# A hybrid token-mixer trunk on one core: four ScalarE operations by head in place of one VectorE operation in layer 0's x scans

## The chip, the core and the metric

One core of one Trainium2 chip. The metric is the device time of one execution in microseconds, the median of several runs. The engines: TensorE (PE; its weight loads are PEld), VectorE (DVE), ScalarE (ACT), GpSimd (POOL) and SyncE (SP), each with a queue of its own that it works off in order.

## What is computed

A trunk of two layers over 512 latent tokens (x) and 256 context tokens (c) of width 1024. A layer normalises, runs four token mixers side by side (pooling, Mamba-2 SSD in both directions, gated DeltaNet in both directions, Fourier), gates and merges them, and then retrieves experts (PEER): 8 heads choose 16 of 16384 single-neuron experts per token. The context goes first; its final states start the scans of x. The two scans, cut to what matters:

```
ssd:   acs    = cumsum(dt * a)                                  # per head, in a chunk
       decay  = exp(where(lower, acs_i - acs_j, -inf))
       y      = (C B^T * decay) (x dt) + C S exp(acs)
delta: gc     = cumsum(g);  decay = exp(where(lower, gc_i - gc_j, -inf))
       a_mat  = where(strict, (k k^T) * decay * beta, 0);  ia = a_mat + I
       u      = solve(ia, v * beta);  w = solve(ia, k * (beta * exp(gc)))
       attn   = (q k^T) * decay;      kdec = k * exp(glast - gc)
       v_new  = u - w S;  o = (q exp(gc)) S + attn v_new;  S = S exp(glast) + kdec^T v_new
```

## The kernel before

All data is fp32 (128 tokens or features on the partitions); the large projections split both operands into a high and a low part and take three matmuls. Instructions are written through the class K; every engine call goes through one helper (line 150), so that line stands for nearly all of the program in a profile and tiles tell the operations apart. A scheduler lays the written operations into the five queues: by priorities, by when it takes inputs and buffers to be ready, and by "sections" that must follow one another. Nobody writes the final order by hand, so an operation that moves to another engine moves others with it.

A layer runs so: the context's projections and scans, then the x tokens' scans, mixing and output projection (mix_out), then the top-k (peer_front), then the experts. The experts of the two context tiles and of one x tile are gathered row by row: GpSimd fetches 128 rows of a table by an indirect DMA into one of four buffers gat (fetch), VectorE multiplies and sums it (the u table, into gdot: gather_u) or scales it and adds it to a sum gacc (the v table: gather_v). The other three x tiles go through all experts as dense matmuls. In layer 0 the context's 512 gathers are a generator (rows) that tick() advances between the steps of the x scans with low priority. What is left of it runs on to the start of the dense part.

The x scans of layer 0 are recurrent(l=0, NT=4). It writes, in this order: the qkv projections, gdn_norm and the token-major keys and values (kt, vt, stored to DRAM as tok), then eight gdn_A, one for each of 4 chunks and 2 directions, whose matrices are inverted block by block in gdn_inv; the xbc projections, ssd_local per chunk and the SSD state steps; and at last eight delta steps, each of gdn_whole (completes the inverse X), gdn_uw and gdn_step.

The diff touches two places. decay makes exp of differences of log decays: a mask is multiplied by the log decays of four heads into R (128 x 4 x 128), a matmul with the other mask sums them, ScalarE takes the exp:

```
R = self.s2((128, 4, 128))
nc.vector.tensor_tensor(R, la[:, :, None].to_broadcast([128, 4, 128]),
                        in_mask[:, None, :].to_broadcast([128, 4, 128]), op=OP.mult)
```

It is called once in gdn_A, four times in ssd_local (2 directions, 2 groups of heads) and once in gdn_uw (each time with the full x scans). gdn_uw multiplies the keys kt by two factors per token and head into ke and kd: by eb = beta exp(gc) and EX for the forward direction, by EX and eb for the other.

In the trace R is s<-la,masks, the key products are s<-s,eb and s<-s,EX (128x512; EX also scales states). In the dense part, it holds the chosen experts' indices, gp their gates, and gates_all compares indices with iota into one-hot B and A, multiplies A by gp (twice) and hands both to TensorE.

Of the kernel before, what the change touches and what calls it, by code (L numbers as in the profile page):

```python
# [17 lines left out]
AF = mybir.ActivationFunctionType  # L18
OP = mybir.AluOpType
# [165 lines left out]
class K:  # L185
# [363 lines left out]
    def norm_steps(self, x, fm, g, s, hT, keep=None):  # L549
        nc = self.nc  # L550
        NT = len(x)
        T = NT * 128
        hh, hl = hT[:, 0], hT[:, 1]
# [84 lines left out]

    def proj_fm(self, src, unit, h, T, fn):

        ps = [self.p()[:, :T] for _ in range(2)]
        for k2 in range(0, 8, 2):
            wh, wl = self.load_w(src[unit, k2 // 4, :, k2 % 4:k2 % 4 + 2])
            for j in range(2):
                for k in range(2):
                    f = slice(j * 128, (j + 1) * 128)
                    self.mm3(ps[j], (wh[:, k, f], wl[:, k, f]), (h[0][k2 + k], h[1][k2 + k]),
                             k2 + k == 0, k2 + k == 7)
        for j in range(2):
            fn(j, ps[j])  # L650
# [13 lines left out]

    def conv_silu(self, l, tile_i, ps, T, bias):

        nc = self.nc
        w = self.vec[l][:, V_CONV + 5 * tile_i:V_CONV + 5 * tile_i + 5]
        u = self.s2((128, T))
        if bias is None:  # L670
            nc.scalar.activation(u, ps, AF.Copy, scale=w[:, 2:3])
        else:
            nc.scalar.activation(u, ps, AF.Identity, scale=w[:, 2:3], bias=bias)
        for k in (0, 1, 3, 4):
            s = k - 2
            a, b = max(0, -s), T - max(0, s)
            nc.vector.scalar_tensor_tensor(u[:, a:b], ps[:, a + s:b + s], w[:, k:k + 1], u[:, a:b],
                                           op0=OP.mult, op1=OP.add)
        th = self.s2((128, T))
        nc.scalar.activation(th, u, AF.Tanh, scale=0.5)  # L680
        nc.vector.scalar_tensor_tensor(u, th, 1.0, u, op0=OP.add, op1=OP.mult)
        return u
# [60 lines left out]
    def decay(self, la, out_mask, in_mask):  # L743

        nc = self.nc
        R = self.s2((128, 4, 128))
        nc.vector.tensor_tensor(R, la[:, :, None].to_broadcast([128, 4, 128]),
                                in_mask[:, None, :].to_broadcast([128, 4, 128]), op=OP.mult)
        ps = self.p((128, 4, 128))
        nc.tensor.matmul(ps, out_mask, R, start=True, stop=True)  # L750
        E = self.s2((128, 4, 128))
        nc.scalar.activation(E, ps, AF.Exp)
        return E

    def dirs(self, d):
        return ((self.LE, self.GT), (self.GE, self.LT))[d]
# [216 lines left out]
    def gdn_uw(self, c, d, X, kt, vt, kf, qf, la, beta, EX, full):  # L973

        nc = self.nc
        tl = slice(c * 128, (c + 1) * 128)
        ei = EX[:, 0, c, 12 * d + 8:12 * d + 12]
        ew = EX[:, 1, c, 12 * d + 8:12 * d + 12]
        b = beta[:, c, 4 * d:4 * d + 4]

        def bc(a):
            return a[:, :, None].to_broadcast([128, 4, 128])
        ke = self.s2((128, 4, 128))
        kd = self.s2((128, 4, 128))
        eb = self.t([128, 4], "eb", 4)
        if d == 0:
            nc.vector.tensor_mul(eb, ei, b)
            vb = self.s2((128, 4, 128))
            nc.vector.tensor_tensor(vb, vt, bc(b), op=OP.mult)
            nc.vector.tensor_tensor(ke, kt, bc(eb), op=OP.mult)  # L990
            nc.vector.tensor_tensor(kd, kt, bc(ew), op=OP.mult)
        else:
            nc.vector.tensor_mul(eb, ew, b)
            vb = vt
            nc.vector.tensor_tensor(ke, kt, bc(ei), op=OP.mult)
            nc.vector.tensor_tensor(kd, kt, bc(eb), op=OP.mult)
        pu = self.p((128, 4, 128))
        pw = self.p((128, 4, 128))
        for h in range(4):
            nc.tensor.matmul(pu[:, h, :], X[:, h, :], vb[:, h, :], start=True, stop=True)  # L1000
            nc.tensor.matmul(pw[:, h, :], ke[:, h, :], X[:, h, :], start=True, stop=True)
        u = self.s2((128, 4, 128))
        w = self.s2((128, 4, 128))
        nc.scalar.copy(u, pu)
        nc.scalar.copy(w, pw)
        if not full:
            return u, w, kd, None
        inc, exc = self.dirs(d)
        pq = self.p((128, 4, 128))
        for h in range(4):  # L1010
            nc.tensor.matmul(pq[:, h, :], kf[h][:, tl], qf[h][:, tl], start=True, stop=True)
        qm = self.s2((128, 4, 128))
        nc.vector.tensor_tensor(qm, pq, inc[:, None, :].to_broadcast([128, 4, 128]), op=OP.mult)
        at = self.decay(la[:, c, 12 * d + 8:12 * d + 12], exc, inc)
        nc.vector.tensor_tensor(at, at, qm, op=OP.mult)
        if d == 1:
            nc.vector.tensor_tensor(at, at, bc(b), op=OP.mult)
        return u, w, kd, at
# [52 lines left out]
    def recurrent(self, l, h, NT, init, full, F, branch):  # L1071

        T = NT * 128
        win = self.io["w_in"][l]
        dt, la, beta, EX = self.scan_scalars(l, h, NT)
        xbc, qkv = {}, {}
# [78 lines left out]
        for n in range(2 * NT):  # L1155
# [3 lines left out]
            with self.section(sec, steps[-SD]) as step:  # L1159
                X = self.gdn_whole(d * NT + c, d, blocks)  # L1160
                kt, vt = (self.get_state(t, 4) for t in tok[c])
# [912 lines left out]
```

## Time and profile before

| | |
|---|---|
| median of 3 runs | 5746.06 us |
| the runs | 5738.55, 5749.92, 5746.06 us |
| profiled execution, its own time | 5736.66 us |
| its span, first to last instruction | 5734.9 us |
| mean granted clock of TensorE | 0.928 |
| busy over the span: PE, DVE, ACT, POOL | 87%, 74%, 34%, 31% |

Windows are in us from the span's start; a busy time is the time in which at least one instruction of the engine ran. A row of a group has the engine, the operation, out<-in with buffer numbers left out, the shapes and the count, then busy us and the mean ns of one, then the idle time in front of it and what ended it. The chain of waits is followed back from the last instruction to what released each step; "issue" in it is time in which the profile shows nothing that was waited for. In a timeline a row has start, duration, engine and operation, and in brackets the idle time ahead of it.

### The profile page before, as it was taken

To read this page: it belongs to the slowest core of one execution; us is meant where nothing else is said; L and a number is where in the kernel's file an instruction comes from. 1 tells how busy PE (TensorE), PEld (TensorE's weight loads), DVE (VectorE), ACT (ScalarE), POOL (GpSimd) and SP (SyncE) were. 2 spreads that over 40 slices of the span, in tenths; PEclk is the share of its full clock that TensorE was granted. 3 is DMA by queue.
4 is the path that set the end of the run, shared out by engine and by line. 5 is a ranking of instruction groups with operands and counts; after the bars stand their busy time and mean duration, and the time that the engine had idled before them with its cause. 6 is when DMAs were issued, how large, how long until landed. Compare 5 with 4: busy or idle time off the path is not lost.

```text
span 5734.9 us, 76857 instructions
## 1 busy us (share of the span) xinstructions
PE 5001.5 (87%) x26902; PEld 4212.1 (73%) x26902; DVE 4267.5 (74%) x7999; ACT 1951.3 (34%) x3711; POOL 1771.4 (31%) x1290
## 2 busy tenths in 40 slices
PE   8998877988467787699999979999888978999997
PEld 3787755763456676699987867787677978999786
DVE  4665777877788889898777786468566488977777
ACT  2444421321003322254333344233134334533333
POOL 0000344333554575644432210000002445443221
PEclk9999989989678898899999989999999989999999
DMA  6555589888878775699889864434334339988897
GB/s 218 176 166 178 166 299 333 268 274 289 286 261 295 243 238 177 223 366 340 298 314 340 317 202 130 127 104 130 125 120 138 126 117 311 364 304 314 316 333 245
DMA packets 618069, 1372.35 MB, mean 239 GB/s; under 512 B 95568, under 2 KB 229328, under 8 KB 614864
## 3 DMA queue, kind: packets, MB, share of 16 engines
q1 hardware_dynamic: 470224, 830.50, 43.5%
q0 software_dynamic: 147456, 536.94, 27.1%
q8 instruction: 211, 3.46, 0.2%
q14 instruction: 178, 1.46, 0.1%
HBM read 1225.64 MB, written 141.56 MB: 238 GB/s over the span
## 4 chain that ended last, share of the span: by engine, by line
PE 55%; DVE 12%; DMA 10%; issue 9%; POOL 5%; ACT 2%; SPq 0%; POOLq 0%; DVEq 0%; ACTq 0%
PE ps L150 39%; PE pa L150 16%; POOL gat L150 4%; DVE s L150 3%; DMA gat<-in_v,gidx 3%; DMA gat<-in_u,gidx 2%; DVE oh L150 1%; DVE gacc L150 1%; DVE gat L150 1%; DMA dv<-in_v 1%; DMA wraw<-in_w_out 1%; POOL dl L150 1%; DMA a<-acts 1%; DMA wraw<-in_w_in 1%; DVE tki L150 1%
## 5 line engine op out<-in xcount | busy, mean ns | idle before, releaser
L150 POOL DMA_INDIRECT gat<-in_v,gidx x512 | 626.8, 1224 | 1063.9 <-DVE gacc L150 924.0
L150 POOL DMA_INDIRECT gat<-in_u,gidx x512 | 684.2, 1336 | 854.1 <-DVE gat L150 783.4
L150 DVE SCALAR_TENSOR_TENSOR gacc<-gat,gact,gacc 128x1024 f32<-128x1024 f32 x508 | 692.7, 1364 | 93.4 <-DMA gat<-in_v,gidx 88.8
L150 PE MATMUL ps<-hx,dh 128*128 128x384 f32 x2944 | 758.8, 338 | 0.0
L150 DVE SCALAR_TENSOR_TENSOR gat<-gat,hb 128x1024 f32<-128x1024 f32 x512 | 629.7, 1241 | 155.8 <-DMA gat<-in_u,gidx 155.2
L150 PE MATMUL ps<-s,s 128*128 128x128 f32 (+3 forms) x2752 | 422.6, 312 | 159.7 <-issue 81.9
L150 PEld LDWEIGHTS ps<-s,s 128*128 128x128 f32 (+1 forms) x2752 | 378.2, 215 | 231.1 <-issue 122.3
L150 PEld LDWEIGHTS ps<-hx,dh 128*128 128x128 f32 x2944 | 534.9, 190 | 5.8
L150 ACT CAST dh<-du 128x1024 fp32r<-128x1024 f32 x256 | 269.2, 1052 | 723.3 <-PE ps L150 405.0
L150 PE MATMUL ps<-hx,dl 128*128 128x384 f32 x1472 | 495.7, 337 | 2.7 <-POOL dl L150 2.6
L150 DVE TENSOR_TENSOR vl<-dv,vh 128x1024 fp32r<-128x1024 f32 x256 | 313.5, 1225 | 206.9 <-ACT vh L150 206.6
L150 ACT CAST xwhi<-xwraw 128x512 fp32r<-128x512 f32 x352 | 217.7, 620 | 519.6 <-PE pa L150 390.8
L150 ACT CAST vh<-dv 128x1024 fp32r<-128x1024 f32 x256 | 269.3, 1052 | 340.1 <-PE ps L150 232.0
L150 PE MATMUL ps<-hx,whi 128*128 128x512 f32 x1152 | 384.1, 401 | 0.0
L150 PE MATMUL pa<-hx,xwhi 128*128 128x512 f32 x1152 | 376.9, 404 | 6.0 <-DVE ld L150 2.9
L150 ACT CAST whi<-wraw 128x512 fp32r<-128x512 f32 x320 | 197.8, 621 | 478.7 <-PE ps L150 306.3
L150 DVE TENSOR_TENSOR xwlo<-xwraw,xwhi 128x512 fp32r<-128x512 f32 x352 | 242.9, 693 | 157.7 <-ACT xwhi L150 144.8
L150 PE MATMUL pa<-hx,dh 128*128 128x384 f32 x1152 | 343.3, 362 | 7.5 <-ACT da L150 7.3
L150 PE MATMUL ps<-vl,gh 128*128 128x512 f32 x1024 | 316.6, 390 | 0.0
L150 PE MATMUL ps<-vh,gl 128*128 128x512 f32 x1024 | 316.1, 390 | 0.0
L150 PE MATMUL ps<-vh,gh 128*128 128x512 f32 x1024 | 316.0, 391 | 0.0
L150 POOL TENSOR_TENSOR dl<-du,dh 128x1024 fp32r<-128x1024 f32 x96 | 250.5, 2611 | 200.5 <-ACT dh L150 183.9
(291 smaller groups left out, 11103.4 us busy)
## 6 DMA issues: line engine op xcount, KB each, us to landing
du<-in_ut SPq DMA_DIRECT2D x256, 512.0 KB, 5.7
dv<-in_v SPq DMA_DIRECT2D x256, 512.0 KB, 5.1
xwraw<-in_w_in SPq DMA_DIRECT2D x272, 256.0 KB, 3.4
wraw<-in_w_in SPq DMA_DIRECT2D x176, 256.0 KB, 3.2
xwraw<-in_w_mod SPq DMA_DIRECT2D x160, 256.0 KB, 4.1
acts<-da SPq DMA_DIRECT2D x176, 192.0 KB, 4.9
rest<-wst SPq DMA_DIRECT2D x48, 704.0 KB, 8.4
W<-rest SPq DMA_DIRECT2D x22, 1536.0 KB, 9.8
```

What stands on the lines that cost most here:

```text
L150: r = f(*a, **kw)
```

## The change

A method by_head multiplies 128 x 4 x 128 by a factor per partition and head. Where self.wide is set (NT is 4 and the layer is 0, thus in layer 0's x scans alone) it is four ScalarE activations, Copy with a scale per partition, one for each head; elsewhere the VectorE operation of before, with its two inputs exchanged. decay uses it for R, gdn_uw for ke and kd. The third product of gdn_uw (vb) stays on VectorE.

```
+    def by_head(self, out, x, w):
+        if self.wide:
+            for h in range(4):
+                self.nc.scalar.activation(out[:, h], x[:, h], AF.Copy, scale=w[:, h:h + 1])
+        else:
+            self.nc.vector.tensor_tensor(out, x, w[:, :, None].to_broadcast([128, 4, 128]), op=OP.mult)
 in decay:
-        nc.vector.tensor_tensor(R, la[:, :, None].to_broadcast([128, 4, 128]),
-                                in_mask[:, None, :].to_broadcast([128, 4, 128]), op=OP.mult)
+        self.by_head(R, in_mask[:, None, :].to_broadcast([128, 4, 128]), la)
 in gdn_uw, d == 0:
-            nc.vector.tensor_tensor(ke, kt, bc(eb), op=OP.mult)
-            nc.vector.tensor_tensor(kd, kt, bc(ew), op=OP.mult)
+            self.by_head(ke, kt, eb)
+            self.by_head(kd, kt, ew)
 else:
-            nc.vector.tensor_tensor(ke, kt, bc(ei), op=OP.mult)
-            nc.vector.tensor_tensor(kd, kt, bc(eb), op=OP.mult)
+            self.by_head(ke, kt, ei)
+            self.by_head(kd, kt, eb)
 in recurrent:
+        self.wide = NT == 4 and not l
```

The queues change as follows. VectorE has 48 operations fewer, ScalarE 192 more (x3 and x4 in a row stand for so many alike). VectorE in one delta step, before (s_3055 is ke, s_3056 is kd, s_3065 is R; TENSOR_SCALAR writes the last block of the inverse):

```order
L150 TENSOR_TENSOR s_3045_12560<-s_3045_12560,ps_12574 128x512
L150 TENSOR_TENSOR s_3058_12605<-s_3054_12599,beta_9514 128x512
L150 TENSOR_TENSOR s_3055_12601<-s_3053_12597,eb_12603 128x512
L150 TENSOR_TENSOR s_3056_12602<-s_3053_12597,EX_9525 128x512
L150 TENSOR_SCALAR s_3045_12560<-ps_12591 64x4x64
L150 SCALAR_TENSOR_TENSOR gacc_12161<-gat_12335,gact_9372,gacc_12161 128x1024
L150 SCALAR_TENSOR_TENSOR gacc_12161<-gat_12338,gact_9372,gacc_12161 128x1024
L150 SCALAR_TENSOR_TENSOR gacc_12161<-gat_12341,gact_9372,gacc_12161 128x1024
L150 TENSOR_TENSOR s_3064_12628<-ps_12623,masks_66 128x512
L150 TENSOR_TENSOR s_3065_12630<-la_9512,masks_66 128x512
```

The same step in the changed kernel:

```order
L150 TENSOR_TENSOR s_3045_12650<-s_3045_12650,ps_12664 128x512
L150 TENSOR_TENSOR s_3058_12695<-s_3054_12689,beta_9514 128x512
L150 SCALAR_TENSOR_TENSOR gacc_12233<-gat_12446,gact_9372,gacc_12233 128x1024
L150 TENSOR_SCALAR s_3045_12650<-ps_12681 64x4x64
L150 SCALAR_TENSOR_TENSOR gacc_12233<-gat_12449,gact_9372,gacc_12233 128x1024
L150 SCALAR_TENSOR_TENSOR gacc_12233<-gat_12452,gact_9372,gacc_12233 128x1024
L150 SCALAR_TENSOR_TENSOR gacc_12233<-gat_12455,gact_9372,gacc_12233 128x1024
L150 TENSOR_TENSOR s_3064_12724<-ps_12719,masks_66 128x512
```

ke, kd and R are gone from the queue; one accumulation of a gathered row has moved in ahead of the TENSOR_SCALAR. This is a forward step; in the four steps of the other direction nothing moves in. ScalarE in the same step, which before held only the copies of 128x512, 64x4x64 and twice 128x512 and the exp:

```order
L150 COPY s_3048_12661<-ps_12656 128x512
L150 ACTIVATE s_3055_12691<-s_3053_12687,eb_12693 128x128 x3
L150 COPY s_3048_12661<-ps_12675 64x4x64
L150 ACTIVATE s_3055_12691<-s_3053_12687,eb_12693 128x128
L150 ACTIVATE s_3056_12692<-s_3053_12687,EX_9525 128x128 x4
L150 COPY s_3061_12715<-ps_12705 128x512
L150 COPY s_3062_12716<-ps_12706 128x512
L150 ACTIVATE s_3065_12726<-masks_66,la_9512 128x128 x4
L150 ACTIVATE s_3067_12733<-ps_12731 128x512
```

The products stand between the step's copies, R between the last copy and the exp. VectorE at the start of layer 0's dense experts, before (gacc rows are the second context tile's last gathers):

```order
L150 CAST iota_19089<-iotaf_70 128x256
L150 SCALAR_TENSOR_TENSOR gacc_13196<-gat_14660,gact_12158,gacc_13196 128x1024
L150 SCALAR_TENSOR_TENSOR gacc_13196<-gat_14663,gact_12158,gacc_13196 128x1024
L150 SCALAR_TENSOR_TENSOR gacc_13196<-gat_14666,gact_12158,gacc_13196 128x1024
L150 SCALAR_TENSOR_TENSOR gacc_13196<-gat_14669,gact_12158,gacc_13196 128x1024
L150 TENSOR_TENSOR B_19163<-it_3960_16154,iota_19089 128x2048
L150 TENSOR_TENSOR A_4557_19165<-it_3959_16153,iota_19089 128x2048
L150 SCALAR_TENSOR_TENSOR gacc_13196<-gat_14672,gact_12158,gacc_13196 128x1024
L150 TENSOR_TENSOR A_4557_19165<-A_4557_19165,gp_16155 128x2048
L150 SCALAR_TENSOR_TENSOR gacc_13196<-gat_14675,gact_12158,gacc_13196 128x1024
L150 TENSOR_TENSOR A_4557_19165<-A_4557_19165,gp_16155 128x2048
```

The same place in the changed kernel (gdot rows are the x tile's first gathers):

```order
L150 CAST iota_19233<-iotaf_70 128x256
L150 SCALAR_TENSOR_TENSOR gat_19270,gdot_19269<-gat_19270,hb_18949 128x1024
L150 TENSOR_TENSOR B_19307<-it_3960_16298,iota_19233 128x2048
L150 TENSOR_TENSOR A_4557_19309<-it_3959_16297,iota_19233 128x2048
L150 TENSOR_TENSOR A_4557_19309<-A_4557_19309,gp_16299 128x2048
L150 SCALAR_TENSOR_TENSOR gat_19313,gdot_19269<-gat_19313,hb_18949 128x1024
L150 TENSOR_TENSOR A_4557_19309<-A_4557_19309,gp_16299 128x2048
```

The context's gathers are no longer here: twelve of them now stand earlier in VectorE's and GpSimd's queues, nine ahead of the first delta step, three within the steps. The x tile's gathers move up by a few rows and keep their place from the sixth B on.

## Rows read from the trace of the kernel before

**Rows 1.** The page: its first line.

```profile
span 5734.9 us, 76857 instructions
```

**Rows 2.** Stretches: from:to, length, busy us (x instructions) of PE, PEld, DVE, ACT, POOL.

```profile
core 0: us, PE busy (x) PEld busy (x) DVE busy (x) ACT busy (x) POOL busy (x), PEclk, DMA share, GB/s
1186.00:1443.00 257.00, 219.79 (x795) 107.50 (x795) 207.11 (x410) 50.87 (x86) 78.05 (x66) 0.94 0.86 291
1443.00:1725.00 282.00, 159.22 (x853) 144.00 (x854) 226.42 (x282) 26.35 (x47) 146.47 (x120) 0.69 0.83 277
2340.00:2367.00 27.00, 19.57 (x101) 18.59 (x102) 24.33 (x21) 5.75 (x8) 22.96 (x14) 0.88 0.87 278
2367.00:2437.00 70.00, 54.02 (x376) 52.27 (x375) 50.56 (x55) 25.20 (x77) 47.05 (x27) 0.85 0.85 278
```

**Rows 3.** Chain of waits by line: 1186 to 1443, 1443 to 1725, 2340 to 2437.

```profile
by line: issue 26.3%; PE ps L150 22.7%; PE pa L150 16.8%; DMA xwraw<-in_w_mod 8.6%; POOL gat L150 7.5%; DMA gat<-in_u,gidx 6.2%; DVE s L150 6.0%; DVE gat L150 5.0%; ACT xs L150 0.7%; ACT s L150 0.5%; DVE wlo L150 0.2%; DVE modfm L150 0.1%; 
...
by line: issue 40.4%; DMA gat<-in_v,gidx 27.5%; POOL gat L150 21.9%; PE ps L150 5.9%; DVE gacc L150 3.2%; DVE s L150 1.5%; POOLq L150 0.4%; DVEq L150 0.0%
...
by line: PE ps L150 24.8%; DMA gat<-in_u,gidx 17.4%; issue 12.1%; DMA gat<-in_v,gidx 11.7%; DVE gacc L150 9.2%; DVE gat L150 8.2%; DVE A L150 6.5%; DVE B L150 4.7%; POOL gat L150 4.3%; POOL dl L150 3.3%; DVE dl L150 2.4%; DVE it L150 0.3%; 
```

**Rows 4.** Groups of VectorE, 1186 to 1725 us.

```profile
L150 DVE SCALAR_TENSOR_TENSOR gacc<-gat,gact,gacc 128x1024 f32<-128x1024 f32 x99 | 126.7, 1280 | 22.3 <-DMA gat<-in_v,gidx 21.0
L150 DVE SCALAR_TENSOR_TENSOR gat<-gat,hb 128x1024 f32<-128x1024 f32 x87 | 104.8, 1219 | 26.2 <-DMA gat<-in_u,gidx 26.2
...
L150 DVE TENSOR_TENSOR s<-s,EX 128x512 f32<-128x512 f32 x32 | 22.1, 690 | 0.0
L150 DVE TENSOR_TENSOR s<-la,masks 128x512 f32<-128x512 f32 x32 | 21.8, 687 | 3.1 <-PE ps L150 3.1
```

**Rows 5.** ScalarE's nearest forms, whole run; the second: min/median/max ns, 990 to 1200.

```profile
L150 ACT ACTIVATE s<-ps 128x512 f32<-128x512 f32 x124 | 74.4, 601 | 180.3 <-PE ps L150 180.1
...
L150 ACT ACTIVATE s<-ps,vec x12: 670/672/690, 1057.9 to 1140.8; 128x512 f32<-128x512 f32 x12
...
L150 ACT ACTIVATE s<-ps,modfm 128x128 f32<-128x128 f32 x112 | 43.4, 474 | 27.3 <-PE ps L150 27.2
...
L150 ACT ACTIVATE s<-s 128x128 f32<-128x128 f32 x18 | 5.3, 297 | 2.5 <-DVE s L150 2.5
```

**Rows 6.** Timeline of one delta step: start us, us, engine, operation.

```profile
1532.86 0.59 ACT L150 COPY s<-ps 128x512 f32<-128x512 f32 x1 [18.53 <-PE ps L150]
...
1542.23 0.69 DVE L150 TENSOR_TENSOR s<-s,EX 128x512 f32<-128x512 f32 x1
...
1542.38 0.37 ACT L150 COPY s<-ps 64x256 f32<-64x256 f32 x1 [8.94 <-PE ps L150]
...
1543.95 0.42 DVE L150 TENSOR_SCALAR s<-ps 64x256 f32<-64x256 f32 x1 [1.03 <-PE ps L150]
...
1547.81 1.07 ACT L150 COPY s<-ps 128x512 f32<-128x512 f32 x2 [5.06 <-PE ps L150]
...
1549.84 0.68 DVE L150 TENSOR_TENSOR s<-la,masks 128x512 f32<-128x512 f32 x1
...
1550.66 1.10 PE L150 MATMUL ps<-s,masks 128*128 128x512 f32 x2 [1.47 <-DVE s L150]
```

**Rows 7.** VectorE's waits, 1443 to 1725 us: us in total, times, longest.

```profile
DVE gacc L150 <- DMA gat<-in_v,gidx: 21.3, 17, 3.0
DVE gat L150 <- DMA gat<-in_u,gidx: 10.5, 7, 4.9
```

**Rows 8.** Start of the dense experts: a group, TensorE's wait, timeline rows, chain.

```profile
L150 DVE SCALAR_TENSOR_TENSOR gacc<-gat,gact,gacc 128x1024 f32<-128x1024 f32 x11 | 18.0, 1635 | 2.7 <-DMA gat<-in_v,gidx 2.6
...
PE ps L150 <- DVE A L150: 20.6, 8, 5.2
...
2341.95 0.28 DVE L150 CAST it<-ps 128x128 f16<-128x128 f32 x1
...
2365.59 1.21 DVE L150 TENSOR_TENSOR A<-A,gp 128x2048 f16<-128x2048 f16 x1
...
2437.57 194.77 PE ps L150 x1518
```

## The prediction

> **What bounds the kernel now.** The profiled execution has a span of 5734.9 us [rows 1]. It took 5736.66 us in all, 9.4 us under the median of 5746.06; sums are made against the profiled execution and carried to the median unchanged. 0.2%, about 11.5 us, is what a measurement of this kernel can tell from no change.
>
> I read the stretches first [rows 2]. The x scans of layer 0 run from 1186 to 1725 us. In their first part (the delta branch's matrices, its inverses, the SSD chunks) TensorE is busy 219.79 of 257 us. In the second (eight delta steps) nobody is full: VectorE 226.42 of 282 us, TensorE 159.22, ScalarE 26.35. ScalarE, which is given the work, has 77 us in 539.
>
> Next the chain of waits, by line [rows 3]. In the first part TensorE's ps and pa groups and the mask-weight loads behind pa make 48%. In the second, the gathers of the context's experts do it: 27.5% a gather in flight, 21.9% GpSimd issuing one, and most of the 40.4% "issue" is a fetch whose buffer VectorE has not yet given back. There are four gather buffers, and VectorE takes its instructions in order, so each scan operation ahead of an accumulation delays the next fetch. 120 fetches left in 282 us (POOL's count in rows 2), one per 2.35 us.
>
> Last, a stretch that no edited line touches: 2340 to 2437 us, where the dense experts of layer 0 begin. There the chain runs through gacc, gat, A and B [rows 3], and TensorE waits 20.6 us for A [rows 8].
>
> **The change, part by part.**
>
> *Removed.* 48 VectorE multiplications of 128x512: 32 masks (8 for gdn_A, 16 for ssd_local, 8 for gdn_uw) and 16 key products. The masks cost 21.8 us for 32, and the products read 690 ns in the EX group [rows 4]; at 0.68 us each the VectorE queue loses 48 x 0.68 = 32.7 us, half of it in either part of the scans (24 masks; 8 masks and 16 products).
>
> *Added.* 192 ScalarE operations of 128x128 with a scale per partition. No row has that form. From below: 297 ns, a 128x128 activation with no such operand. From above: 474 ns, one with a scale and a bias that also reads PSUM. A scale per partition makes a 128x512 operation 672 instead of 601 ns, so 297 + 71 = 368 ns is the value nearest in form, and I take it: 1.47 us for four [rows 5], between 1.19 and 1.90. That is 71 us more on ScalarE (57 to 91), on top of 77 busy in 539. The Trainium skill, in "ScalarE: Activation LUTs", section "What ACT_TABLE_LOAD costs", has a price for the form; an estimate by it is 186 + 93 + 0.833 x 128 = 386 ns, 1.54 us for four, and the sum would stand as it is.
>
> *Is ScalarE ever last?* I cost it at nothing on the path. In the step shown [rows 6] it copies at 1532.86 and next at 1542.38; three heads of the first product and, behind the second copy, the rest (1 + 4 heads, 1.8 us, ready at 1544.6) stand between there and the copies at 1547.81. TensorE can't use them before the small VectorE operation of 1543.95. The mask follows these copies, which end at 1548.88, and is ready at 1550.4; now VectorE makes it at 1549.84 and TensorE uses it at 1550.66. Behind the new operations ScalarE's queue holds the small 64-row copy and the Exp; if a key tile came late, both would wait, and TensorE's correction of the inverse behind them. The mask's inputs are ready long before, and the key product waits for a tiny VectorE factor that stands well ahead.
>
> *First part of the scans: 0 us.* 24 masks leave VectorE (16.4 us), and by the orders nine more u gathers come in (243 instead of 234 before the first step's factors), 9 x 1.219 = 11.0 us [rows 4]. What is left, 5 us, lies beside a TensorE-led chain. Ends: 5 us less; or, if the nine fit in no gap, 9 x 2.35 = 21 us more.
>
> *Delta steps: 6 us less.* 24 operations leave (16.4 us). In four of the eight steps a gather takes the place of the two key products, so three to four more gathers run (3 x 1.28 = 3.8 us). In the other four nothing takes the place of the pair, and VectorE waits there for the small TensorE product anyway, as after 1542.23, where 1.03 us were idle already [rows 6]: 4 x 1.37 = 5.5 us turn into waiting. 16.4 - 3.8 - 5.5 = 7.1 us remain. VectorE also waits 31.8 us for gathers in flight [rows 7], a wait that grows when it arrives earlier, so I take 6. Ends: 12.6 less (all but the three gathers), 3 x 2.35 = 7 more.
>
> *Between 1725 and 2330 us: 0.* The lead of 12 gathers persists through the output projection and the top-k. The switch from the first context tile's sum to the second moves forward by these 12, to between eight short scalings; its wait for the store of that sum is as long as now.
>
> *Start of the dense experts: 12 us less.* From the last lookup of the top-k on, the old order has 18 context gathers, the new one 6, all of them ahead of it (2341.95 in the trace). The 12 that go stand from there on, around B and A; 11 accumulations of this stretch take 18.0 us [rows 8], so VectorE can be up to 12 x 1.635 = 19.6 us earlier at the second A. TensorE can't follow all of it: of 27 us it is busy 19.57, in the next 70 us 54.02 [rows 2], idle 23.4 us together, of which A is the reason for 20.6. The x tile's first gather moves in front of B and may have to be waited for. I take about half of the 23.4. Ends: 0 (its own gathers make A as late) and 20.6.
>
> *Beyond 2437 us: 0.* From there the chain stays 194.77 us on TensorE without a piece of anything else [rows 8], and everything shifts along.
>
> Sum: 0 - 6 - 12 = 18 us less: 5736.7 - 18 = 5719 for the profiled execution, **5728** against the median. With all good ends 5 + 12.6 + 20.6 = 38 less, with all bad ones 28 more.
>
> **Rivals.**
>
> *A, no change.* The gather pipeline sets the pace of the scans: VectorE's freed time goes into waiting for data, and the 12 gathers brought forward cost some 10 us there, which the dense start gives back: 5744. For it: the transfers' share is 0.86 and 0.83 in both parts [rows 2]. Against: 2.35 us per fetch, where VectorE waits only 31.8 of 282 us for data.
>
> *B, slower.* ScalarE's factors become the last arrival before the masks' and key products' matmuls. Each of the 48 then takes 1.47 instead of 0.68 us on the path, 48 x 0.79 = 38 more, less 12 at the dense start: 5772. It decides once ScalarE's queue holds more than the gap between two of its copies (8.94 us idle before 1542.38 [rows 6]), likeliest in gdn_A, where eight masks and eight Exp alternate. Against: 51 of 257 us busy there. The Trainium skill's "ScalarE: Activation LUTs", section "Rules for kernel authors", speaks for this rival: it gives multiplications to VectorE, not to ScalarE. No row here has both engines at the same multiplication.
>
> *C, all of it.* VectorE's place in the queue is the whole pace of scans and dense start: 38 less, 5708.
>
> That only the intended scans change is in the order: 48 operations fewer on VectorE, and elsewhere the rows only swap the names of two operands.
>
> **How the numbers follow.** Forecast 0.45, A 0.27, B 0.13, C 0.15. Faster by over 0.2%: C and nearly all of the forecast, 0.58. Within 0.2%: the rest of the forecast and most of A, 0.28. Slower: B and a tail of A, 0.14. The range goes from C, 5708, to 5757, where A's scans lose 21 us and half is given back; B lies outside. The likeliest case's own range is 5716 to 5738.
>
> **What would show it.** In the profile after: 192 ScalarE operations of 128x128 near 0.37 us; VectorE's mask groups down by 32; the delta steps some 6 us shorter; from it to the first A some 10 us less, and TensorE's wait for A well under 20.6 us. Wrong would be: TensorE waiting for ScalarE in the scans (B), or scans longer by about what the dense start gains, with VectorE's wait for gathers well over 31.8 us (A).

## The result and the profile after

The changed kernel takes 5764.73 us (median of 8 runs, 5753.91 to 5780.31), the kernel before 5736.76 (8 runs, 5726.13 to 5749.92): a ratio of 1.0053, interval 1.0042 to 1.0064, 28 us between the medians and **slower** where 18 less were forecast. The median that the forecast started from, 5746.06 us of three runs, lies 9.3 us above that of the eight; the time lies above the range given all the same. The profiled execution, 5753.91 us, is the shortest of the eight: it shows 17 us of the loss, the rest has no trace.

Where the time went is read between instructions that stand on VectorE in both kernels. *Matrices*: from the first product of gdn_A (s<-s,beta,ps) to the copy that ends the inverses. *Chunks*: from there to the first eb<-EX,beta. *Steps*: to the eighth eb. *Top-k*: to the cast of iota. *Dense*: to the seventh B. In brackets VectorE's gather operations in the stretch. Each row of this table and the next is one execution. How far a stretch varies by itself can be read where two executions have the same program there: the steps by 4.0 us between e9 and e18 and 3.1 between the kernel before and e12 (whose edit is in layer 1), the chunks by 0.7 and 1.6, the matrices by 1.8 and 0.1, the dense start by 2.7 and 1.8.

| us | first product | matrices | chunks | steps | top-k | dense |
|---|---|---|---|---|---|---|
| before | at 1194.5 | 109.1 | 139.6 (43) | 219.5 (93) | 684.0 | 97.5 |
| after | at 1192.3 | 117.5 | 166.1 (52) | 219.5 (96) | 677.4 | 92.3 |
| difference | -2.2 | +8.4 | +26.5 | 0.0 | -6.6 | -5.2 |

That is 20.8 us more by 2465 us; the remaining 3.6 of the profile's 17.2 come back later, nowhere in one place. The loss lies ahead of the first delta step.

The page and the stretches of the changed kernel, each shifted with its work, as [rows 1, 2]:

```profile
span 5752.1 us, 77016 instructions
```

```profile
1186.00:1476.00 290.00, 231.57 (x801) 114.64 (x799) 204.41 (x406) 78.52 (x179) 83.66 (x76) 0.89 0.81 276
1476.00:1758.00 282.00, 159.79 (x847) 143.82 (x848) 216.59 (x250) 54.56 (x143) 146.27 (x124) 0.68 0.84 283
2370.00:2397.00 27.00, 19.72 (x99) 19.34 (x100) 12.96 (x13) 5.75 (x8) 16.05 (x9) 0.82 0.59 201
2397.00:2458.00 61.00, 51.46 (x377) 50.09 (x376) 44.91 (x51) 24.95 (x77) 35.90 (x21) 0.90 0.78 254
```

ScalarE is busy 78.5 of 290 us in the first part: it is far from full. The larger part of its new operations, and VectorE's gathers from 1186 to 1758, as [rows 4, 5]:

```profile
L150 ACT ACTIVATE s<-masks,la 128x128 f32<-128x128 f32 x128 | 40.8, 395 | 0.0
L150 ACT ACTIVATE s<-s,eb 128x128 f32<-128x128 f32 x32 | 10.6, 392 | 4.3 <-DMA s<-tok 4.3
```

```profile
L150 DVE SCALAR_TENSOR_TENSOR gacc<-gat,gact,gacc 128x1024 f32<-128x1024 f32 x111 | 142.2, 1281 | 32.0 <-DMA gat<-in_v,gidx 28.5 <-issue 2.2
L150 DVE SCALAR_TENSOR_TENSOR gat<-gat,hb 128x1024 f32<-128x1024 f32 x87 | 105.4, 1221 | 48.0 <-DMA gat<-in_u,gidx 47.3 <-issue 0.4
```

One has 0.395 us on record, but those in a row overlap: four take 1.27 us (below). VectorE waits 47.3 us for u rows, 26.2 before, and 28.5 for v rows, 21.0 before. At the dense start TensorE waits 16.6 us for A, 20.6 before [rows 8]:

```profile
PE ps L150 <- DVE A L150: 16.6, 5, 6.7
```

ScalarE in gdn_A of the changed kernel (start, us):

```profile
1196.10 0.60 ACT L150 ACTIVATE s<-ps 128x512 f32<-128x512 f32 x1 [0.29 <-PE ps L150]
1196.60 1.26 ACT L150 ACTIVATE s<-masks,la 128x128 f32<-128x128 f32 x4
1199.86 0.60 ACT L150 ACTIVATE s<-ps 128x512 f32<-128x512 f32 x1 [2.00 <-PE ps L150]
1200.35 1.26 ACT L150 ACTIVATE s<-masks,la 128x128 f32<-128x128 f32 x4
1203.61 0.60 ACT L150 ACTIVATE s<-ps 128x512 f32<-128x512 f32 x1 [2.00 <-PE ps L150]
1204.11 1.26 ACT L150 ACTIVATE s<-masks,la 128x128 f32<-128x128 f32 x4
1218.35 1.29 ACT L150 CAST whi<-wraw 128x512 fp32r<-128x512 f32 x2 [12.98 <-DMA wraw<-in_w_in]
1219.55 0.59 ACT L150 ACTIVATE s<-ps 128x512 f32<-128x512 f32 x1
1220.04 1.26 ACT L150 ACTIVATE s<-masks,la 128x128 f32<-128x128 f32 x4
```

s<-ps is the Exp, s<-masks,la the R of the next matrix. R needs nothing from the Exp ahead of it, but stands behind it in an in-order queue, and the Exp waits for TensorE, which waits for the R before. So Exp, R and matmul take turns. One matrix takes 3.75 us (1199.86 to 1203.61); that holds four matmuls of the modulation (pa<-xwraw,sc, 1.88 us), which end 0.9 us after R is ready. Where none stands between, mask matmul follows mask matmul after 2.97 us, TensorE idle for R, and after 1.86 in the kernel before; changed kernel, then before:

```profile
1202.45 1.12 PE L150 MATMUL ps<-s,masks 128*128 128x512 f32 x2
1205.42 1.13 PE L150 MATMUL ps<-s,masks 128*128 128x512 f32 x2 [0.96 <-ACT s L150]
```

```profile
1208.91 1.12 PE L150 MATMUL ps<-s,masks 128*128 128x512 f32 x2
1210.77 1.02 PE L150 MATMUL ps<-s,masks 128*128 128x512 f32 x2
```

Then a cast waits 12.98 us for a weight with an Exp and the last two R behind it; TensorE's next mask matmul comes after 13.91 us idle:

```profile
1221.36 2.07 PE L150 MATMUL ps<-s,masks 128*128 128x512 f32 x2 [13.91 <-ACT s L150]
```

In the matrices TensorE waits 14.9 us for R in all; in the chunks only 4.6 us, three times.

### The profile page after: what moved, and what is told of

Same layout as the page of the kernel before. It is cut to its first block, busy times and chain, and to the rows that moved or that the text cites. A ratio compares the mean times of both kernels' runs of the same rounds, so it can differ in the third digit from the quotient of the medians.

```text
span 5752.1 us, 77016 instructions
## 1 busy us (share of the span) xinstructions
PE 5000.8 (87%) x26902; PEld 4210.2 (73%) x26902; DVE 4233.8 (74%) x7951; ACT 2006.8 (35%) x3903; POOL 1748.6 (30%) x1290
## 3 DMA queue, kind: packets, MB, share of 16 engines
q14 instruction: 180, 1.47, 0.1%
## 4 chain that ended last, share of the span: by engine, by line
PE 54%; DVE 12%; issue 11%; DMA 8%; POOL 6%; ACT 2%; SPq 0%; POOLq 0%; DVEq 0%; ACTq 0%
PE ps L150 39%; PE pa L150 15%; POOL gat L150 5%; DMA gat<-in_v,gidx 3%; DVE s L150 3%; DVE oh L150 2%; DMA gat<-in_u,gidx 2%; DVE gacc L150 1%; DVE gat L150 1%; DMA dv<-in_v 1%; DMA wraw<-in_w_in 1%; DMA wraw<-in_w_out 1%; ACT xs L150 1%; DVE tki L150 1%; POOL dl L150 0%
## 5 line engine op out<-in xcount | busy, mean ns | idle before, releaser
L150 POOL DMA_INDIRECT gat<-in_v,gidx x512 | 615.2, 1202 | 1071.8 <-DVE gacc L150 934.4
L150 PEld LDWEIGHTS ps<-s,s 128*128 128x128 f32 (+1 forms) x2752 | 386.0, 219 | 238.5 <-issue 108.1
```

The source lines that it names most:

```text
L150: r = f(*a, **kw)
```

## The experiments

Theories: **queue place** (R stands behind an Exp that waits for TensorE), **price** (ScalarE is slower at the same product and last on the path: rival B), **gathers** (the twelve that were brought forward are the loss: rival A's scans). "Three places", an early form, put the loss on the weight, on ScalarE being last in the SSD chunks, and on gathers. All runs but e12 (its loss is in layer 1), stages as above, ratio to the kernel before:

| run | matrices | chunks | steps | dense | ratio (95%) |
|---|---|---|---|---|---|
| e1 VectorE, no gathers | 92.8 | 111.5 (0) | 156.3 (0) | | |
| e2 ScalarE, no gathers | 95.0 | 143.5 (0) | 152.7 (0) | | |
| e5 same, SSD masks ahead | 94.1 | 98.4 (0) | 159.7 (0) | | |
| e3 VectorE, gathers earlier | 108.0 | 146.4 (49) | 224.2 (93) | 88.2 | 0.9998 (0.9988, 1.0009) |
| e4 change, gathers later | 117.8 | 157.4 (45) | 217.6 (93) | 100.0 | 1.0033 (1.0019, 1.0048) |
| e6 change, SSD masks ahead | 113.4 | 124.9 (40) | 229.0 (97) | 96.1 | 0.9999 (0.9987, 1.0011) |
| e7 without SSD masks | 115.0 | 142.3 (46) | 219.7 (95) | 89.0 | 1.0009 (0.9997, 1.0021) |
| e8 SSD masks only | 109.2 | 164.7 (50) | 217.4 (92) | 90.3 | 1.0027 (1.0012, 1.0042) |
| e9 e6, zeros early | 107.4 | 132.2 (40) | 228.4 (97) | 91.4 | 0.9985 (0.9974, 0.9997) |
| e18 e9 again | 109.2 | 132.9 (40) | 232.4 (97) | 94.1 | 0.9998 (0.9987, 1.0009) |
| e10 e6, gdn_A on VectorE | 108.1 | 131.7 (40) | 228.4 (98) | 99.9 | 1.0012 (1.0002, 1.0022) |
| e11 VectorE, SSD masks ahead | 108.3 | 114.5 (30) | 224.7 (93) | 120.7 | 1.0001 (0.9988, 1.0013) |
| e13 e6, gdn_A ahead too | 106.7 | 135.0 (40) | 234.9 (98) | 100.0 | 1.0005 (0.9990, 1.0020) |
| e14 e13, zeros early | 101.9 | 132.8 (41) | 236.3 (97) | 101.6 | 1.0008 (0.9996, 1.0019) |
| e15 VectorE, zeros early | 105.7 | 140.4 (45) | 216.9 (93) | 92.5 | 0.9996 (0.9985, 1.0007) |
| e16 change, zeros early | 107.2 | 170.5 (52) | 218.4 (96) | 93.2 | 1.0044 (1.0026, 1.0061) |
| e17 SSD masks only, ahead, zeros early | 103.5 | 126.1 (40) | 225.7 (93) | 104.0 | 0.9994 (0.9983, 1.0006) |

### The gathers taken away (e1, e2, e5)

e1 is the kernel before, e2 the change, both with:

```
-TL = 510
+TL = 174
 in tick:
+        if not n:
+            return
 in ticked:
+            self.held = self.mark
 in run:
-                self.run_all(rows)
+                with self.section(self.held):
+                    self.run_all(rows)
```

> The kernel before, with its context gathers held back until layer 0's x scans and merges are written (174 of 512 ahead of the scans, none within them). It is the partner of the next run, and is read by stages: the x scans should be well shorter than before (539 us), the whole run longer, since 185 gathers more come behind them. No theory hangs on it alone.

> The same with the change (factors on ScalarE). No gather can move into the scans here, so only the engine of the 48 products differs. Gathers alone (the 12 gathers that the scheduler brought forward are the whole loss): scans equal to the partner's or up to 15 us shorter. ScalarE last (each of the 48 is the last arrival): scans 25 to 40 us longer. Three places (a weight cast ahead of two masks of gdn_A, ScalarE last in the SSD chunks, gathers in the later chunks): 5 to 20 us longer up to the first delta step, delta steps equal or a few us shorter.

e5 is e2 with the masks of a chunk written ahead:

```
 in ssd_local, ahead of the loop over directions (decay takes R as an argument):
+        if full and self.wide:
+            for d in range(2):
+                for g in range(2):
+                    Rs[d, g] = self.s2((128, 4, 128))
+                    self.by_head(Rs[d, g], inc of d, la of d, g)
```

> No gathers in the scans, factors on ScalarE, but the four R of an SSD chunk are written ahead of the chunk's other work, so that none stands behind an Exp in ScalarE's queue. To be read by stages against the two earlier runs without gathers (first SSD product of the first chunk to the first delta step: 96 us with VectorE, 117 with ScalarE). Queue place (each R waits in ScalarE's queue behind the Exp before it, which waits for TensorE): the chunks go back to the length with VectorE, 96 us within 5. Price alone (ScalarE's 1.27 us against VectorE's 0.64 on a chain that has it last): at least 16 x 0.63 = 10 us of the 21 stay.

With no gather to move, the change still makes the chunks 32 us longer; so gathers alone are out. Up to the first step e2 is 30 us behind e1, up to the eighth 26: what price said (25 to 40), and more than three places said (5 to 20). Over the whole run it is 15.5 us (5958.06 against 5942.53). The steps are 3.6 us shorter, which is within what one program's steps differ by. e5, run once (5931.60 us), makes the same sixteen operations per chunk on the same engine, and the chunks fall to 98.4 us, 13 below VectorE's; from the first chunk's y to the first step it is 80.8 us (expected 96 within 5, or at least 106). That is shorter than either theory said, and price alone is out as well. ScalarE in one half chunk (copy of the state, two Exp, and R), e1, e2 and e5:

```profile
1337.13 0.59 ACT L150 COPY s<-ps 128x512 f32<-128x512 f32 x1 [4.38 <-PE ps L150]
1340.00 0.60 ACT L150 ACTIVATE s<-ps 128x512 f32<-128x512 f32 x1 [2.28 <-PE ps L150]
...
1342.06 0.60 ACT L150 ACTIVATE s<-ps 128x512 f32<-128x512 f32 x1 [0.49 <-PE ps L150]
```

```profile
1358.34 0.59 ACT L150 COPY s<-ps 128x512 f32<-128x512 f32 x1 [4.38 <-PE ps L150]
1358.82 1.28 ACT L150 ACTIVATE s<-masks,la 128x128 f32<-128x128 f32 x4
...
1361.31 0.60 ACT L150 ACTIVATE s<-ps 128x512 f32<-128x512 f32 x1 [0.75 <-PE ps L150]
1361.80 1.26 ACT L150 ACTIVATE s<-masks,la 128x128 f32<-128x128 f32 x4
1365.37 0.60 ACT L150 ACTIVATE s<-ps 128x512 f32<-128x512 f32 x1 [2.30 <-PE ps L150]
```

```profile
1335.48 4.77 ACT L150 ACTIVATE s<-masks,la 128x128 f32<-128x128 f32 x16
...
1340.88 0.58 ACT L150 COPY s<-ps 128x512 f32<-128x512 f32 x1 [0.17 <-ACT xs L150]
1341.69 0.60 ACT L150 ACTIVATE s<-ps 128x512 f32<-128x512 f32 x1 [0.23 <-PE ps L150]
1342.55 0.60 ACT L150 ACTIVATE s<-ps 128x512 f32<-128x512 f32 x1 [0.26 <-PE ps L150]
```

From Exp to Exp: 2.06 us with R on VectorE, 4.06 with R between them, 0.86 with both R ahead. The 4.06 are not all waiting: the scheduler put six of the modulation's matmuls (2.74 us) into them, and two into the 2.06. What the chunks' 32 us are is read from TensorE over the whole stretch, e1, e2, e5 (columns as [rows 2], the granted clock third from the end), and from its wait for R in e2:

```profile
1288.60:1400.10 111.50, 106.53 (x399) 44.78 (x398) 61.01 (x108) 22.05 (x40) 0.00 (x0) 0.98 0.49 148
1286.60:1430.20 143.60, 129.28 (x438) 53.50 (x437) 55.55 (x101) 42.91 (x108) 0.00 (x0) 0.89 0.46 142
1292.50:1391.00 98.50, 91.38 (x374) 44.28 (x373) 54.22 (x96) 40.81 (x105) 0.00 (x0) 1.00 0.46 137
```

```profile
PE ps L150 <- ACT s L150: 9.2, 6, 1.8
```

In e2 TensorE is idle 9 us longer than in e1 (14.3 against 5.0), about what it waits for R, and busy 23 us longer. 12 of these are modulation matmuls (65.5 us of them in the chunks against 53.4), which e1 does in other stretches; some 11 are the chunks' other products at a lower granted clock, 0.89 against 0.98 (last section). e5 has 40.9 us of modulation matmuls in its chunks, 12.5 less than e1: nearly all of the 13 us by which its chunks are shorter. So a stretch's length alone is no loss or gain; work that can stand elsewhere moves in and out of it.

### Moving gathers without the change, and back (e3, e4)

```
 e3, in the kernel before:  -GP = 3000   +GP = 2000
 e4, in the change:         -RT = (20,8,2,8,21,21,9)   +RT = (20,8,2,4,21,21,9)
```

> The kernel before, multiplications on VectorE, but the gathers' priority is raised (GP 2000 for 3000), which brings 6 of them ahead of the first delta step (240 where it was 234; the change has 243) and leaves 4 fewer for the dense start. Gathers alone: two thirds of the change's loss, 15 to 20 us slower than before. Three places: 6 x 2.35 = 14 more in the scans less some 3 to 5 at the dense start, 5 to 12 us slower. ScalarE last: no difference, within 5 us.

> The change, with 4 instead of 8 gathers released after each SSD chunk: 236 ahead of the first delta step (before 234, change 243), 500 ahead of the dense start (before 503). All 48 products stay on ScalarE. Gathers alone: back to the time before, within 5 us. Three places: 7 x 2.35 = 16 us of the 28 come back in the scans, some 9 are lost again at the dense start, so 15 to 25 us slower than before. ScalarE last: 28 us slower, as the change.

Six gathers more in e3's chunks cost 6.8 us there, and the dense start gives back 9.3: over all nothing, which speaks against "gathers alone" and "three places" (price had said no difference). In e4 seven fewer give 8.7 us back in the chunks, and the dense start is 7.7 longer; 1.0033 is 19 us, what "three places" said, and rules out gathers alone (within 5); its interval, 11 to 28 us, does not tell three places from price (28). A gather moved costs about 1.1 to 1.2 us in the chunks, not 2.35.

### Which masks, and their place (e6 to e8)

e6 is the change with the edit of e5. e7 and e8 give by_head a tag:

```
 e7: +        if self.wide and tag in ('A', 'uw', 'ke', 'kd'):
 e8: +        if self.wide and tag in ('ssd',):
```

> The change with the same edit and with its gathers (231 ahead of the first delta step, 504 ahead of the dense start; before 234 and 503). Queue place: the 28 us of the change go, and its gains in the steps stay: 0 to 10 us faster than before. Price alone: 10 to 20 us slower than before. Gathers alone: within 5 us of before.

> The change for gdn_A and the delta steps alone; the 16 masks of ssd_local are on VectorE as before. Queue place: the chunks go as before, the 13 us wait for a weight in gdn_A and the gain of the steps about cancel: within 6 us of before. Price alone: 32 of 48 products, 15 to 20 us slower than before. Gathers alone (237 against 234, 507 against 503): 5 to 8 us slower.

> The reverse: only the 16 masks of ssd_local on ScalarE, gdn_A and the steps as before. Queue place: the loss is here, 20 to 30 us slower up to the first delta step and 15 to 28 us over all. Price alone: 16 of 48, 8 to 10 us. Gathers alone (241 against 234, 507 against 503): 10 to 16 us.

In e6 all 48 products stay on ScalarE, the masks of the chunks are written in another place, and the loss is gone (0.9999). Price misses e6 (10 to 20 us slower) and e7 (15 to 20; 1.0009 with 32 of the 48). But with the masks' place other things moved: e6 has 12 gathers fewer in the chunks than the change, and 17.1 us of modulation matmuls in the delta steps, where the change and the kernel before have none. "Gathers alone" said e6 and e7 as well; it is e2 and e5, with no gathers, and e8 that rule it out. e8 alone makes the chunks 25.1 us longer, as the change does (26.5), with as many modulation matmuls there as before (125 and 125); its 7 gathers more at 1.2 us would be 8 of the 25. The chunks' window, before and in e8:

```profile
1303.60:1443.20 139.60, 115.47 (x412) 45.85 (x410) 108.50 (x192) 21.46 (x38) 52.61 (x43) 0.95 0.86 286
1304.10:1468.80 164.70, 128.44 (x412) 54.13 (x410) 107.07 (x191) 39.79 (x102) 59.80 (x50) 0.87 0.78 265
```

TensorE does the same 412 matmuls in 13 us more, at a granted clock of 0.87 instead of 0.95, and is idle 12 us more. So about half of the 25 us is idle time, and half is the same matmuls taking longer at the lower clock.

### gdn_A and its weight (e9, e10, e13 to e16)

```
 zeros early (e9, e14, e15, e16), in recurrent, layer 0's x scans:
+        self.zeros(2 * NT)
         dt, la, beta, EX = self.scan_scalars(l, h, NT)
 e10, in gdn_A:
+        old, self.wide = self.wide, False
         E = self.decay(...)
+        self.wide = old
 e13, in inverses, in the loop over the matrices i:
+        for j in range(i, min(i + 3, 8)):
+            if j not in Rs: Rs[j] = s2; self.by_head(Rs[j], ...)
```

> The change with its SSD masks written ahead, and the 16 stores of zeros (dx, dxt) that stand in SyncE's queue ahead of gdn_A's weight loads written at the start of the scans. Store queue (the weight arrives late because its load stands behind these stores; ScalarE's cast of it waits 12 to 13 us with two masks and their Exp behind it): the wait falls under 4 us, gdn_A (first to last matrix) from 35.5 to 25 us or less, and the run is 5 to 12 us faster than before. Otherwise (the load itself is slow, or its buffer comes free late): the wait and the time stay as they are without the edit, within 5 us of before.

> The change with its SSD masks written ahead, and gdn_A's eight masks back on VectorE. Queue place: gdn_A takes 27 us again instead of 35.5, and the run is 4 to 10 us faster than before. If the gathers' pace takes up whatever is gained ahead of the delta steps, as it did with masks written ahead alone: within 5 us of before.

> The change with all masks written ahead: those of the SSD chunks as before, and each R of gdn_A two matrices ahead. Queue place: gdn_A takes 25 us or less (before 26.7, change 36.5), and the run is 0 to 10 us faster than before, as far as the gathers' pace leaves it. Price alone: gdn_A stays at 33 to 36 us and the run within 5 us of before.

> The same with the stores of zeros written early. Queue place: gdn_A 25 us or less, 8 to 15 us faster than before. If the gain of the earlier run with the zeros early was that of the zeros alone, this one is no faster than the kernel before with them.

> The kernel before, factors on VectorE, with the stores of zeros written at the start of the scans. If the zeros alone gave the gain: 5 to 12 us faster than before. If they matter only where ScalarE's queue waits for the weight: within 4 us of before (that wait is 3.2 us there).

> The change as it is, with the stores of zeros written early and nothing else. If the wait for the weight carries a part of the 28 us: 5 to 10 us of it go, 18 to 23 us slower than before. If it is taken up by the gathers' pace: 28 us slower, as the change.

zeros(G) is the part of gdn_blocks that stores the 16 blocks of zeros. With it early the cast's wait is 5.3 us where it was 12.2 in e6, so the stores ahead of the load are part of it; but from the first to the last matrix it is still 32.9 us (expected under 4 and 25 or less: both missed). e13 shows why: with R ahead the eight take 12.2 us, and 26.7 on VectorE. ScalarE in e13:

```profile
1194.11 0.58 ACT L150 ACTIVATE s<-ps 128x512 f32<-128x512 f32 x1
1194.59 1.27 ACT L150 ACTIVATE s<-masks,la 128x128 f32<-128x128 f32 x4
1195.76 0.58 ACT L150 ACTIVATE s<-ps 128x512 f32<-128x512 f32 x1
1196.23 1.27 ACT L150 ACTIVATE s<-masks,la 128x128 f32<-128x128 f32 x4
```

No wait is left, and a matrix takes 1.65 us. But other work of TensorE that stood between the matrices now stands behind them, and matrices and inverses together are 106.7 against 109.1. e10 has the eight back on VectorE: 26.9 us from the first to the last matrix as said, but 1.0012 over all, where 4 to 10 us less were expected. e14, with R ahead and the zeros early, is 1.0008 where 8 to 15 us less were expected. So no mending of gdn_A showed a gain over all. How much of the change's loss the weight carries stays open: in e16, the change with zeros early, the cast's wait is 7.0 us and the matrices are 107.2 us, 10 less than in the change, but the chunks are 4 us longer, and its 1.0044 (1.0026 to 1.0061) fits the change's loss as well as one 10 us smaller. The zeros alone (e15) give 0.9996.

### Does any placing win? (e11, e12, e17, e18)

```
 e11: the edit of e5 in the kernel before, R by VectorE's operation
 e12: e6 with  self.wide = NT == 4 and l == 1
 e17: e9 with self.wide True in ssd_local alone
```

> The kernel before, all on VectorE, with the SSD chunk's four R written ahead of the chunk in layer 0's x scans. It has 13 gathers fewer ahead of the steps (221 against 234) and 13 fewer ahead of the dense start (490 against 503). If writing ahead is the gain, whatever the engine: up to the first delta step 8 us or more shorter than before. If it only undoes the queue place on ScalarE: the chunks are as before or shorter by the gathers that are missing, and the dense start longer; over all within 8 us of before.

> The change, with masks written ahead, in layer 1's x scans instead of layer 0's (there no gathers run beside them). Queue place: with VectorE's queue shorter and no gathers, the scans get shorter as in the run without gathers (chunks 15 us), unless TensorE is the bound there (it is 88 to 97% busy in these stretches): between 10 us faster than before and no change. Price alone: 10 to 25 us slower.

> Of the change only the 16 SSD masks, written ahead, on ScalarE, with the stores of zeros early; gdn_A and the steps on VectorE. 231 gathers ahead of the steps (before 234), 498 ahead of the dense start (503). Chunks 10 us or more shorter than before; the gathers that are pushed out are paid for at 2.35 us each in the steps and at the dense start: within 6 us of before over all. If the steps' factors had carried the gain of the earlier run: no gain here; if they cost: faster than it, 10 us or more below before.

> The run with SSD masks ahead and zeros early once more. If its gain is real: 4 to 12 us faster than before again. If it was chance: within 3 us.

No. e9's 0.9985 came back as 0.9998 in e18. e11 has shorter chunks, 25.1 us, with 13 gathers fewer in them, and pays 23.2 at the dense start, where VectorE has those gathers ahead of A. At 1.1 to 1.2 us a gather some 15 of the 25 are gathers, so about 10 come from writing ahead on VectorE too. Over all the four kernels make a square: R in its old place 1.0053 with ScalarE against the kernel before, the chunks' R ahead 1.0001 with VectorE (e11) and 0.9999 with ScalarE (e6). A difference between the engines can be told only in the old place. e6, e13 and e14 gain in the chunks (15, 5 and 7 us) and lose in the steps (9.5, 15 and 17), where 97 or 98 gathers stand instead of 93. There are also 17.1, 14.4 and 17.0 us of modulation matmuls in their steps, where before there are none; no run tells the two apart.

e12 is 1.0023 (1.0012 to 1.0034) in layer 1, worse than queue place said and within what price said (10 to 25 us). At the last product of gdn_A it is 3.1 us ahead of the kernel before, at the first eb 6.7 behind. Its trace shows the same fault in another place: the sixteen operations of a chunk's R, written ahead, stand in one row in front of a weight cast; VectorE waits for the cast, and TensorE for a product behind that in VectorE's queue:

```profile
3936.56 4.78 ACT L150 ACTIVATE s<-masks,la 128x128 f32<-128x128 f32 x16
3941.23 0.61 ACT L150 CAST xwhi<-xwraw 128x512 fp32r<-128x512 f32 x1
...
3941.87 0.69 DVE L150 TENSOR_TENSOR xwlo<-xwraw,xwhi 128x512 fp32r<-128x512 f32 x1 [3.91 <-ACT xwhi L150]
...
3945.64 2.04 PE L150 MATMUL ps<-s,s 128*128 128x256 f32 x4 [4.71 <-DVE s L150]
```

The granted clock is 0.71 and 0.86 in the two windows from 3940 to 3956, 1.00 in both before. No run moves these sixteen, so this is read, not shown.

## Why the prediction was wrong

**"Is ScalarE ever last? I cost it at nothing on the path"** is the step that failed. It was read in one delta step [rows 6], and nothing speaks against it there: without gathers the steps are no longer with ScalarE (152.7 us against 156.3). It was then carried to gdn_A and ssd_local, where decay is called again and again and R follows the Exp of the call before. "The mask's inputs are ready long before" was true and beside the point: in the queue it stood behind an operation whose input was not.

**First part, 0 us (5 less to 21 more): measured 33 more** up to the first eb. The upper end took only the nine gathers in; ScalarE was not in it. Nine more gathers at 1.1 to 1.2 us are about 10 of it. The rest, some 23, goes with R's place in the queue: 8.4 us in the matrices, with the cast's wait, and the larger part of the 26.5 in the chunks, by TensorE's idle time and the clock that fell with it, as e8 shows for the chunks' masks alone.

**Rival B** had the sign and named gdn_A and its alternation of masks and Exp, but its mechanism was price (0.79 us on the path each, 38 in all) and its condition a queue with more work than the gap between two copies. ScalarE had 78.5 us in 290. The condition is order, not load. The prediction's bad ends add up to 28 us more (21, 7 and 0), outside its own range. That this meets the measured 28 is chance: those three stages came as 33 more, 0 and 9 less.

**Added, 1.47 us for four:** 1.27 measured, within 1.19 to 1.90. Each has 391 to 395 ns on record, next to the 386 worked out by the Trainium skill's "ScalarE: Activation LUTs", section "What ACT_TABLE_LOAD costs". The same section of the Trainium skill has operations in a row overlap by about 93 ns, which the prediction's 1.54 us for four left out: an estimate with it is 4 x 386 - 3 x 93 = 1265 ns, and the trace agrees. The rule of the same page of the Trainium skill to give multiplications to VectorE (section "Rules for kernel authors") would have had the sign, but e6 has all 48 on ScalarE and no loss.

**Steps, 6 less: 0.0 measured**, where one program's steps differ by up to 4 us. Three gathers came in, as said; they were costed at 1.28 us each, VectorE's own time. The steps run at 219.5 / 93 = 2.36 us per gather before and 2.29 in the change, so three are some 7 us and could take the gain; that was named as the bad end. e4 bears it out, as far as one trace can: the same products on ScalarE, 93 gathers as before, and 217.6 us. So the pace goes by the gathers, which is rival A's mechanism.

**1725 to 2330, 0: 6.6 less** between the eighth eb and iota, partly the last step itself.

**Dense start, 12 less: 9.1 less** (29.9 us behind at the last lookup, 20.8 later), near in size, but not as told. The first A, which was to come some 10 us earlier, is 3.0 later after the lookup, because the x tile's gather in front of B has to be waited for:

```profile
2386.53 4.08 DVE L150 SCALAR_TENSOR_TENSOR gat<-gat,hb 128x1024 f32<-128x1024 f32 x1 [13.45 <-DMA gat<-in_u,gidx]
```

That was named, as what would make the gain 0. The first B is 35.0 us behind the kernel before, the fourth 21.2: the gain comes there, where the kernel before still has five of the context's gathers between its B and A. **Beyond, 0: 3.6 less.**

**"Wrong would be: TensorE waiting for ScalarE in the scans (B), or scans longer by about what the dense start gains, with VectorE's wait for gathers well over 31.8 us (A)":** the first came in gdn_A (13.91 us at one mask matmul). Of the second the wait came, 40.3 us for gathers from 1476 to 1758, but the scans are 33 us longer and 9.1 are gained, so A is not the account.

## What to carry to other kernels

When an operation moves to another in-order queue, look at what it will stand behind, not only at how busy the engine is: an operation that depends on nothing, behind one that waits for a third engine, joins two independent chains into one. Where a helper makes, multiplies and exponentiates in one call, write the independent first part of several calls ahead before moving it, but look again at what then stands behind the row (e12). And in a stretch with filler work at its own pace, count the pieces that move in or out at that pace before a saving is booked; where other work can fill a gap, as the modulation's matmuls do here, compare whole runs and not one stretch.

## What was not expected of the hardware

TensorE's clock made the first chunk dearer. Windows of the changed kernel from the end of the inverses, columns as [rows 2] (granted clock third from the end):

```profile
1308.00:1316.00 8.00, 6.98 (x21) 1.99 (x20) 3.19 (x8) 2.52 (x7) 0.00 (x0) 1.00 0.83 198
1316.00:1324.00 8.00, 4.14 (x13) 1.29 (x12) 3.18 (x7) 3.93 (x11) 0.00 (x0) 1.00 0.53 88
1324.00:1332.00 8.00, 6.15 (x16) 3.55 (x16) 1.99 (x3) 2.35 (x6) 0.00 (x0) 0.50 0.52 177
1332.00:1340.00 8.00, 8.00 (x35) 7.53 (x35) 3.31 (x6) 0.58 (x2) 1.21 (x1) 0.50 0.00 0
1340.00:1348.00 8.00, 6.44 (x17) 1.67 (x16) 6.74 (x13) 1.44 (x6) 4.93 (x5) 0.93 0.72 240
```

TensorE is busy 4.14 of 8 us while it takes turns with ScalarE, then the clock is 0.50 (1.2 of 2.4 GHz) in the next two windows; before, it is 1.00 in all windows from 1292 to 1372. The chunk's products, after and before:

```profile
1329.73 7.88 PE L150 MATMUL ps<-s,s 128*128 128x64 f32 x34
```

```profile
1315.71 4.48 PE L150 MATMUL ps<-s,s 128*128 128x64 f32 x34 [0.39 <-DVE s L150]
```

The same 34 take 3.4 us longer. And ScalarE's small operations cost less in a row: 0.395 us for one, 1.27 for four, 4.77 for sixteen, so each behind the first adds 0.29 us.
